# The old columns of a packed inverse: added by VectorE in strips, instead of through a product with the identity

## The chip, the cores and the metric

One core of a Trainium2 chip runs the whole program. The metric is the device time of one execution in microseconds, and kernels are compared by the median of several executions.

## The reference

The kernel computes one decoder layer with two groups of heads: four heads of gated delta-rule linear attention, and four heads of differential attention. The change lies in the first group. Its sequence of 2048 positions is cut into chunks (64 in the reference, 128 in the kernel, which gives the same result), and each chunk needs a unit lower triangular system solved:

```python
m = jnp.where(strict, jnp.einsum('bhncd,bhnsd->bhncs', k_beta, kc) * decay, 0.0)
lmat = m + jnp.eye(CHUNK, dtype=m.dtype)
rhs = jnp.concatenate([v_beta, k_beta * jnp.exp(gc)[..., None]], axis=-1)
sol = lax.linalg.triangular_solve(lmat, rhs, left_side=True, lower=True,
                                  unit_diagonal=True)
u, w = sol[..., :dv], sol[..., dv:]
```

Then a scan over the chunks carries the state, and the outputs of both groups go through one output projection and are added to the input.

## The kernel before, in words

The program has two stages. In the first, `feed` (L878) issues the input projections (tiles `pct` and `pnat`, each of 24 products of split operands, L365 and L384), while `gdn` (L909) runs the delta-rule units: `gdn_unit` (L596) prepares one head for 512 positions, that is four chunks of 128, and `gdn_scan` (L802) carries the state through them. There are 16 units in two chains, `gg` 0 and 1, which run side by side. `mingle` (L137) lays some steps of the projections between any two steps of the units. In the second stage `attention` (L1166) runs the differential attention, mingled with the output projection (`outp`). From what is written, a scheduler with a clock of its own makes the order in which each engine gets its instructions; each engine then takes them strictly in that order. Every matmul is recorded at L130 and every transpose at L133, so they are told apart by their tiles.

A unit inverts its four unit triangular 128x128 matrices `L` by doubling: it starts with the inverses of 2x2 blocks, and each level joins pairs of blocks into blocks of twice the size. At a level, only the odd half of each pair's columns of `N` (the inverse so far, transposed) changes: the new columns are the old ones, plus a correction. Levels 1 to 4 (block sizes 2, 4, 8 and 16) stay within diagonal blocks of 32x32 and are computed *packed*: the 16 diagonal blocks of the four chunks are gathered into one 128x128 tile, `Nc` for `N` and `Lc` for `L`, where partition strip m of 32 holds the m-th diagonal blocks of all four chunks. For each packed level (L722 to L750):

- `xq` (L734): one product of `Lc` with the odd columns `No` of the full `N`, 256 columns; VectorE masks it into `X` (L736).
- `nq` (L739, L740): two products of 256 columns into the same PSUM tile. The first, with the identity `identr` as stationary operand, copies `No` into it; the second adds the correction, `TT` times `X` (`TT` is the packed `N` transposed). The mask's sign makes the correction negative.
- VectorE writes `No` from `nq`, times a mask that keeps the diagonal blocks (L741, 128x256), and ScalarE copies the four strips of `nq` into `Nc` (L744, four copies of 32x64), except at the last packed level.
- `tp` (L707): `Nc` is transposed and ScalarE copies it to `TT` for the next level (L709). After the last packed level the four chunks of `N` itself are transposed (L715, L717), for the two wide levels that follow.

The PSUM tiles `xq`, `nq` and `tp` of a chain are one buffer (`ua`, L316), so each waits until the one before it has been read.

The two lines that compute the old columns:

```python
PE.matmul(blocks(np_), lhsT=identr, rhs=No, start=True, stop=False)
PE.matmul(np_, lhsT=TT[:, 0, :], rhs=X, start=False, stop=True)
```

Of the kernel before, what the change touches and what calls it, by code (L numbers as in the profile page):

```python
# [13 lines left out]
ALU = mybir.AluOpType  # L14
AX = mybir.AxisListType

P = 128
# [6 lines left out]
NCH = 4  # L24
# [43 lines left out]
LEVELS = [1, 2, 4, 8, 16, 32, 64]  # L68


WIDE = (0, 5, 6)
PACKED = (1, 2, 3, 4)
PK = 32
NM = len(WIDE) * P + (len(PACKED) + 1) * 2 * P


def level_masks():

    s = np.arange(P)[:, None]
    c = np.arange(P)[None, :]  # L80

    def level(b, s, c):
        return (s // (2 * b) == c // (2 * b)) & (s // b % 2 == 0) & (c // b % 2 == 1)

    m = [level(LEVELS[i], s, c).astype(np.float32) for i in WIDE]
    j, k, i = np.meshgrid(np.arange(4), np.arange(4), np.arange(16), indexing="ij")
    for n in PACKED:
        b = LEVELS[n]
        col = (i // b * 2 * b + b + i % b).reshape(-1)[None, :]
        m.append(-((s // PK == j.reshape(-1)[None, :]) & level(b, s % PK, col)).astype(np.float32))  # L90
    m.append((s // PK == k.reshape(-1)[None, :]).astype(np.float32))
    return np.ascontiguousarray(np.concatenate(m, 1))


def f(ap):
    return ap.bitcast(F32)
# [3 lines left out]
def hybrid_kernel(  # L100
# [21 lines left out]
    V, A, PL, SY = nc.vector, nc.scalar, nc.gpsimd, nc.sync  # L122
# [12 lines left out]
    PE = Recorder()  # L135

    def mingle(a, b, rate, slack=0, drain=True):  # L137

        credit = 0.0
        steps = [None] * (slack + 1)  # L140
        done = object()
        while a or (b and drain):
            last[0] = None
            r = next(a, done) if a else "wait"
            if last[0]:
                steps = steps[1:] + last
            step = steps[0]
            credit = rate[0] if r else credit + rate[0]
            q = None
            while b and (credit > 0 or not a) and not q:  # L150
                with tc.issue_after(step.ins) if step else ExitStack():
                    q = next(b, done)
                credit -= 1.0
            assert not (r == "wait" and q == "wait"), "stuck"
            a = None if r is done else a
            b = None if q is done else b
        return b
# [90 lines left out]
    identr = const.tile([P, P], F32R, name="identr")  # L248
# [4 lines left out]
    PL.affine_select(utri, ones, pattern=[[1, P]], compare_op=ALU.is_ge, fill=0.0, base=0, channel_multiplier=-1)  # L253
    lmask = const.tile([P, NM], F32, name="lmask")
    ab = const.tile([P, 2, H], F32, name="ab")
# [60 lines left out]
    def ua(gg, name, dt=F32):  # L316
        return psg.tile([P, NCH, P], dt, tag=f"ua{gg}", name=name, bufs=1)
# [278 lines left out]
    def gdn_unit(h, g):  # L596
# [3 lines left out]
        s = {k: a[:, h, 4 * gg : 4 * gg + 4] for k, a in sc[hf].items()}  # L600

        def t(tag, name, dt=F32, shape=S4):
            return gp.tile(shape, dt, tag=f"u{gg}_{tag}", name=f"u{gg}_{name}")
# [40 lines left out]
        b = gp.tile([P, NCH], F32, tag="l_b", name="b", bufs=3)  # L644
# [45 lines left out]
        N = t("c", "N", F32R)  # L690
# [4 lines left out]
        Nc = t("Nc", "Nc", F32R, [P, NCH, PK])  # L695
        strips = [slice(PK * m, PK * m + PK) for m in range(NCH)]
# [4 lines left out]
        def flat(a):  # L701
            return a.rearrange("p a b -> p (a b)")

        def transposed_packed():

            tp = ua(gg, "tp", F32R)
            PE.transpose(tp[:, 0, :], flat(Nc), identr)  # L707
            TT = t("d", "TT", F32R)
            A.copy(TT[:, 0, :], f(tp[:, 0, :]))  # L709
            return TT  # L710

        def transposed(N):
            tp = ua(gg, "tp", F32R)
            for j in range(NCH):
                PE.transpose(tp[:, j, :], N[:, j, :], identr)  # L715
            TT = t("d", "TT", F32R)
            A.copy(TT, f(tp))  # L717
            return TT

        TT = transposed_packed()  # L720
        yield
        for i in PACKED:  # L722


            def half(a, lvl=LEVELS[i]):
                return a.rearrange("p (m two b) -> p m two b", two=2, b=lvl)[:, :, 1, :]

            def blocks(a, lvl=LEVELS[i]):
                return a.rearrange("p (m b) -> p m b", b=lvl)

            No = half(flat(N))
            off = len(WIDE) * P + PACKED.index(i) * 2 * P
            xp_ = flat(ua(gg, "xq")[:, :2, :])
            PE.matmul(blocks(xp_), lhsT=flat(Lc), rhs=No, start=True, stop=True)  # L734
            X = flat(t("e", "X", F32R)[:, :2, :])
            V.tensor_tensor(X, xp_, lmask[:, off : off + 2 * P], op=ALU.mult)  # L736
            yield
            np_ = flat(ua(gg, "nq")[:, :2, :])
            PE.matmul(blocks(np_), lhsT=identr, rhs=No, start=True, stop=False)  # L739
            PE.matmul(np_, lhsT=TT[:, 0, :], rhs=X, start=False, stop=True)  # L740
            V.tensor_tensor(No, blocks(np_), blocks(lmask[:, NM - 2 * P :]), op=ALU.mult)  # L741
            if i < PACKED[-1]:
                for m, r in enumerate(strips):
                    A.copy(  # L744
                        Nc.rearrange("p j (m two b) -> p j m two b", two=2, b=LEVELS[i])[r, :, :, 1, :],
                        np_.rearrange("p (j k m b) -> p j k m b", j=NCH, k=NCH, b=LEVELS[i])[r, :, m],
                    )
            yield
            TT = transposed_packed() if i < PACKED[-1] else transposed(N)
            yield  # L750
        for i in WIDE[1:]:

            def odd(a):
                return a.rearrange("p j (m two b) -> p j m two b", two=2, b=LEVELS[i])[:, :, :, 1, :]
# [4 lines left out]
            No = odd(N)  # L759
# [4 lines left out]
            X = t("e", "X", F32R)[:, :, :HC]  # L764
            V.tensor_tensor(blocks(X), blocks(xp_), odd(lm(i)), op=ALU.mult)
            yield
            np_ = ua(gg, "np")[:, :, :HC]
# [4 lines left out]
            TT = transposed(N)  # L772
# [136 lines left out]
    def gdn():  # L909


        def chain(gg):
            for hf in range(2):
                for h in range(H):
                    n = 8 * hf + 2 * h + gg
                    while ready[0] <= n or scanned[0] < n - 2:
                        yield "wait"
                    yield from gdn_unit(h, 2 * hf + gg)
# [413 lines left out]
    b = mingle(gdn(), behind(), pace, SLACK, drain=False)  # L1332
# [34 lines left out]
```

## Time and profile before

| | |
|---|---|
| median of 3 runs | 1680.2 us (1675.32 to 1682.49) |
| the profiled execution's own time | 1688.5 us |
| its span, first to last instruction | 1686.8 us |
| mean granted TensorE clock | 0.976 of full speed |
| instructions | 27350 |

The profiled execution is a run of its own, 0.5% above the median of the others; durations and waits are taken from it. Engines are named PE (TensorE's matmuls), PEld (its weight loads), DVE (VectorE), ACT (ScalarE), POOL (GpSimd) and SP. A row names an instruction by line, engine, operation and the tiles out<-in, where the numbers of tiles are left out: `u_N` is `N` of a unit of either chain. A matmul's duration in a row overlaps that of its neighbours; what it takes of TensorE's time is the step from its start to the next one's.

### The profile page before, as it was taken

How to read it: one execution, taken by the hardware profiler on the slowest of the kernel's cores; microseconds unless marked ns; L12 is line 12 of the kernel's file. 1: busy time of each engine (PE TensorE's matmuls, PEld its weight loads, DVE VectorE, ACT ScalarE, POOL GpSimd, SP SyncE). 2: the span in 40 equal slices, each digit the busy share in tenths (PEclk: the TensorE clock that was granted, in tenths of full speed). 3: DMA queues.
4: the chain of work that ended last, by engine and by line, in shares of the span. 5: the costliest groups of instructions: out<-in, count | busy, mean ns of one | idle time of the engine just before them, and what ended most of it. 6: DMA issues, size and time to landing. Idle time of an engine off the chain costs nothing.

```text
span 1686.8 us, 27350 instructions
## 1 busy us (share of the span) xinstructions
PE 1584.1 (94%) x9388; PEld 1374.7 (82%) x9388; DVE 1067.4 (63%) x2435; ACT 788.4 (47%) x2409; POOL 697.7 (41%) x846
## 2 busy tenths in 40 slices
PE   5999999999998999999999999889999989998997
PEld 4888898888987988898889898678778767777876
DVE  3765666746444684756654543338888768888872
ACT  4444444343345444334434343337777555565540
POOL 2464375352352347257442352213333353443343
PEclk8999999999999999999999999899999989999999
DMA  7342245233336432424422322896653364743344
GB/s 171 74 101 63 54 86 124 51 96 56 77 99 134 83 92 72 73 57 107 107 59 73 49 71 70 195 265 199 185 150 112 114 175 132 187 137 108 98 159 156
DMA packets 187703, 188.51 MB, mean 112 GB/s; under 512 B 12978, under 2 KB 143148, under 8 KB 187564
## 3 DMA queue, kind: packets, MB, share of 16 engines
q1 hardware_dynamic: 187564, 186.76, 43.6%
q8 instruction: 74, 1.21, 0.3%
q14 instruction: 65, 0.53, 0.1%
HBM read 124.82 MB, written 61.90 MB: 111 GB/s over the span
## 4 chain that ended last, share of the span: by engine, by line
PE 73%; DVE 10%; DMA 7%; ACT 3%; POOL 3%; issue 2%; SPq 1%; DVEq 0%; ACTq 0%; POOLq 0%
PE pct L130 25%; PE pnat L130 13%; PE outp L130 8%; PE oT L130 6%; PE sp L130 5%; PE wtp L133 2%; DVE nm L1024 2%; DMA u_gcr<-gc_d 2%; DMA wor<-in_w_out_dram 2%; DVE ex L1078 1%; PE gqp L130 1%; PE op L130 1%; PE ysp L130 1%; ACT ex L1026 1%; DVE qkraw L510 1%
## 5 line engine op out<-in xcount | busy, mean ns | idle before, releaser
L1026 ACT ACTIVATE ex<-sp,nm 128x512 f32<-128x512 f32 (+3 forms) x320 | 198.5, 625 | 100.2 <-DVE nm L1024 82.4
L130 PE MATMUL outp<-wo,mt 128*128 128x512 f32 x720 | 205.7, 416 | 10.8 <-ACT wo L1203 5.2
L1024 DVE TENSOR_REDUCE nm<-sp 128x1 f32<-128x512 f32 (+3 forms) x320 | 186.8, 602 | 26.4 <-PE sp L130 24.8
L130 PE MATMUL sp<-k,qs 128*128 128x512 f32 (+3 forms) x640 | 184.3, 393 | 19.0 <-ACT ex L1026 17.9
L130 PEld LDWEIGHTS outp<-wo,mt 128*128 128x128 f32 x720 | 130.2, 192 | 35.7 <-ACT wo L1203 5.9
L130 PE MATMUL pnat<-wh_fqk,xh 128*128 128x256 f32 (+1 forms) x512 | 152.9, 300 | 5.5 <-DVE xl L342 2.5
L130 PE MATMUL pnat<-wl_fqk,xh 128*128 128x256 f32 (+1 forms) x512 | 151.4, 297 | 1.3 <-POOL wl_fqk L361 1.3
L130 PE MATMUL pnat<-wh_fqk,xl 128*128 128x256 f32 (+1 forms) x512 | 150.5, 295 | 0.0
L130 PEld LDWEIGHTS sp<-k,qs 128*128 128x128 f32 x640 | 107.5, 191 | 47.9 <-ACT ex L1026 35.2
L1074 POOL TENSOR_SCALAR ex<-ex,al 128x512 f32<-128x512 f32 (+3 forms) x140 | 94.5, 691 | 95.6 <-ACT al L1035 92.3
L130 PE MATMUL oT<-wt,v 128*128 128x256 f32 (+1 forms) x576 | 132.6, 374 | 1.4 <-ACT wt L1084 1.4
L564 DVE SCALAR_TENSOR_TENSOR cy<-craw,cc,cy 128x512 f32<-128x512 f32 x144 | 124.0, 862 | 3.3
L130 PEld LDWEIGHTS oT<-wt,v 128*128 128x128 f32 x576 | 108.3, 193 | 17.7 <-ACT wt L1084 2.4
L1078 DVE SCALAR_TENSOR_TENSOR ex<-ex,cf 128x512 f32<-128x512 f32 (+3 forms) x160 | 111.2, 739 | 9.7 <-ACT cf L1053 9.2
L130 PEld LDWEIGHTS pnat<-wh_fqk,xh 128*128 128x128 f32 x512 | 100.7, 197 | 7.5 <-issue 2.6
L130 PE MATMUL pct<-xh,wh_dvz 128*128 128x512 f32 x256 | 104.1, 407 | 0.0
L130 PE MATMUL pct<-xl,wh_dvz 128*128 128x512 f32 x256 | 103.5, 404 | 0.0
L130 PE MATMUL pct<-xh,wl_dvz 128*128 128x512 f32 x256 | 103.5, 405 | 0.0
L130 PEld LDWEIGHTS pnat<-wl_fqk,xh 128*128 128x128 f32 x512 | 100.9, 197 | 2.3 <-POOL wl_fqk L361 1.7
L130 PE MATMUL pct<-xh,wh_dqk 128*128 128x512 f32 x256 | 102.3, 399 | 0.0
L130 PE MATMUL pct<-xl,wh_dqk 128*128 128x512 f32 x256 | 102.1, 399 | 0.0
L130 PEld LDWEIGHTS pnat<-wh_fqk,xl 128*128 128x128 f32 x512 | 100.9, 197 | 0.3
(280 smaller groups left out, 4132.4 us busy)
## 6 DMA issues: line engine op xcount, KB each, us to landing
qs<-qst_d SPq DMA_DIRECT2D x128, 128.0 KB, 3.8
mt<-mx_d SPq DMA_DIRECT2D x48, 256.0 KB, 4.8
k<-kst_d SPq DMA_DIRECT2D x40, 256.0 KB, 6.2
wr_dqk<-in_w_in_dram SPq DMA_DIRECT2D x32, 256.0 KB, 5.0
wr_dvz<-in_w_in_dram SPq DMA_DIRECT2D x32, 256.0 KB, 6.0
qst_d<-qkhl SPq DMA_DIRECT2D x16, 512.0 KB, 2.8
kst_d<-qkhl SPq DMA_DIRECT2D x16, 512.0 KB, 7.8
part_d<-xr SPq DMA_DIRECT2D x32, 256.0 KB, 4.1
```

The lines of the kernel that those rows point to most:

```text
L130: last[0] = nc.tensor.matmul(*a, **k)
L133: last[0] = nc.tensor.transpose(*a, **k)
L510: V.tensor_tensor(rv, rv, bc(r[:, j].unsqueeze(2), [P, 4, 64]), op=ALU.mult)
L564: V.scalar_tensor_tensor(y, raw[:, j : j + G], convc[:, j, idx : idx + 1], y, op0=ALU.mult, op1=ALU.add)
L1024: V.tensor_reduce(mx, sp[:, :w], axis=AX.X, op=ALU.max, negate=True)
L1026: A.activation(e[:, :w], sp[:, :w], AF.Exp, bias=mx, accum_out=ss[:, m, pi : pi + 1])
L1074: PL.tensor_scalar(e0[:, :w], e0[:, :w], al[:, 0, pi : pi + 1], 1.0, op0=ALU.mult, op1=ALU.mult)
L1078: V.scalar_tensor_tensor(e1[:, :w], e1[:, :w], cf[:, pi : pi + 1], e0[:, :w], op0=ALU.mult, op1=ALU.add)
```

## The change

The identity product and the block mask are gone. Now `nq` holds the correction alone, and VectorE adds it, strip by strip, to the packed `Nc` in place: four instructions of 32x64 at every packed level, the last one too. Then ScalarE copies the four strips from `Nc` into the odd columns of the full `N`, again four instructions of 32x64, at every packed level. So the transposition of `Nc` waits for VectorE instead of ScalarE, and whatever reads `N` (the next level's `xq`, and after the last packed level the four transposes of `N`) waits for the ScalarE copies that stand behind VectorE's adds. The mask table is 256 columns narrower.

```diff
--- before.py
+++ after.py
@@ -71,7 +71,7 @@
 WIDE = (0, 5, 6)
 PACKED = (1, 2, 3, 4)
 PK = 32
-NM = len(WIDE) * P + (len(PACKED) + 1) * 2 * P
+NM = len(WIDE) * P + len(PACKED) * 2 * P
 
 
 def level_masks():
@@ -83,12 +83,11 @@
         return (s // (2 * b) == c // (2 * b)) & (s // b % 2 == 0) & (c // b % 2 == 1)
 
     m = [level(LEVELS[i], s, c).astype(np.float32) for i in WIDE]
-    j, k, i = np.meshgrid(np.arange(4), np.arange(4), np.arange(16), indexing="ij")
+    j, _, i = np.meshgrid(np.arange(4), np.arange(4), np.arange(16), indexing="ij")
     for n in PACKED:
         b = LEVELS[n]
         col = (i // b * 2 * b + b + i % b).reshape(-1)[None, :]
         m.append(-((s // PK == j.reshape(-1)[None, :]) & level(b, s % PK, col)).astype(np.float32))
-    m.append((s // PK == k.reshape(-1)[None, :]).astype(np.float32))
     return np.ascontiguousarray(np.concatenate(m, 1))
 
 
@@ -736,15 +735,17 @@
             V.tensor_tensor(X, xp_, lmask[:, off : off + 2 * P], op=ALU.mult)
             yield
             np_ = flat(ua(gg, "nq")[:, :2, :])
-            PE.matmul(blocks(np_), lhsT=identr, rhs=No, start=True, stop=False)
-            PE.matmul(np_, lhsT=TT[:, 0, :], rhs=X, start=False, stop=True)
-            V.tensor_tensor(No, blocks(np_), blocks(lmask[:, NM - 2 * P :]), op=ALU.mult)
-            if i < PACKED[-1]:
-                for m, r in enumerate(strips):
-                    A.copy(
-                        Nc.rearrange("p j (m two b) -> p j m two b", two=2, b=LEVELS[i])[r, :, :, 1, :],
-                        np_.rearrange("p (j k m b) -> p j k m b", j=NCH, k=NCH, b=LEVELS[i])[r, :, m],
-                    )
+            PE.matmul(np_, lhsT=TT[:, 0, :], rhs=X, start=True, stop=True)
+
+            for m, r in enumerate(strips):
+                nb = np_.rearrange("p (j k m b) -> p j k m b", j=NCH, k=NCH, b=LEVELS[i])[r, :, m]
+                c = Nc.rearrange("p j (m two b) -> p j m two b", two=2, b=LEVELS[i])[r, :, :, 1, :]
+                V.tensor_tensor(c, f(c), nb, op=ALU.add)
+            for r in strips:
+                A.copy(
+                    N.rearrange("p j (m two b) -> p j m two b", two=2, b=LEVELS[i])[r, :, r.start // (2 * LEVELS[i]) : r.stop // (2 * LEVELS[i]), 1, :],
+                    f(Nc).rearrange("p j (m two b) -> p j m two b", two=2, b=LEVELS[i])[r, :, :, 1, :],
+                )
             yield
             TT = transposed_packed() if i < PACKED[-1] else transposed(N)
             yield
```

How the orders move. In these pieces names carry the scheduler's numbers where they tell units apart; `u0` and `u1` are the two chains.

On TensorE, around the first packed level of the chain-0 unit of the second head (`nq` at 240.2 us of the trace). Before:

```order
L133 MATMUL qktp<-ident,qkraw 128x128
L130 MATMUL pnat<-wh_fqk_0_2255,xl_411 128x256
L130 MATMUL pnat<-wh_fqk_0_2255,xh_410 128x256
L130 MATMUL nq<-u_N,identr 128x256
L130 MATMUL nq<-u_X,u_TT 128x256
L130 MATMUL pnat<-wl_fqk_0_2256,xh_410 128x256
```

Now:

```order
L132 MATMUL qktp<-ident,qkraw 128x128
L129 MATMUL pnat<-wh_fqk_0_2279,xl_411 128x256
L129 MATMUL pnat<-wh_fqk_0_2279,xh_410 128x256
L129 MATMUL nq<-u_X,u_TT 128x256
L129 MATMUL pnat<-wl_fqk_0_2280,xh_410 128x256
```

The identity product is gone and nothing takes its place; the projections around it close up.

On TensorE, at the last packed level of the chain-1 unit of the third head (403 to 406 us of the trace). Before:

```order
L133 MATMUL tp_4577<-identr_171,u0_N_4181 128x128 x4
L130 MATMUL nq_4567<-u1_N_4215,identr_171 128x256
L130 MATMUL nq_4567<-u1_X_4539,u1_TT_4520 128x256
L130 MATMUL pct_4631<-xh0_221,wh_dvz3_0_4360 128x512
...
L130 MATMUL pct_4631<-xl0_222,wh_dvz3_0_4364 128x512
L133 MATMUL tp_4589<-identr_171,u1_N_4215 128x128 x4
```

Now:

```order
L129 MATMUL pct_4629<-xh1_410,wl_dqk3_0_4406 128x512
L129 MATMUL nq_4633<-u1_X_4599,u1_TT_4580 128x256
L129 MATMUL pct_4703<-xh0_221,wh_dvz3_0_4412 128x512
...
L129 MATMUL pct_4703<-xh0_221,wl_dvz3_0_4413 128x512
L132 MATMUL tp_4649<-identr_171,u0_N_4229 128x128 x4
L129 MATMUL pct_4703<-xh0_221,wh_dvz3_0_4416 128x512
...
L129 MATMUL pct_4703<-xl0_222,wh_dvz3_0_4416 128x512
L132 MATMUL tp_4661<-identr_171,u1_N_4263 128x128 x4
```

The left-out rows are projection products: eleven of them stood between the level's product and the four transposes of the unit's `N`, and now eleven and the four transposes of the other chain's `N`, which stood ahead of the product before.

On ScalarE, around 271 us of the trace, where a chain-0 unit is at its last packed level and the chain-1 unit at its first two. Before:

```order
L744 CAST u_Nc<-nq 32x32x2 x4
L500 COPY qkraw<-pnat 128x256
L709 CAST u_TT<-tp 128x128
L500 COPY qkraw<-pnat 128x256
L360 CAST wh_dqk_0_3262<-wr_dqk_0_3259 128x2x256
L479 ACTIVATE qkhl<-qktp,qg 128x512
L744 CAST u_Nc<-nq 32x16x4 x4
L500 COPY qkraw<-pnat 128x256
L717 CAST u_TT<-tp 128x512
```

Now:

```order
L745 CAST u_N<-u_Nc 32x4x8x2 x4
L499 COPY qkraw<-pnat 128x256
L708 CAST u_TT<-tp 128x128
L499 COPY qkraw<-pnat 128x256
L745 CAST u_N<-u_Nc 32x4x16 x4
L499 COPY qkraw<-pnat 128x256
L745 CAST u_N<-u_Nc 32x4x4x4 x4
L359 CAST wh_dqk_0_3304<-wr_dqk_0_3301 128x2x256
L478 ACTIVATE qkhl<-qktp,qg 128x512
L716 CAST u_TT<-tp 128x512
```

Copies out of `nq` (L744) have become copies from `Nc` to `N` (L745) at the same places, and a block of four more (`32x4x16`, the last packed level) stands ahead of the copy `u_TT` of 512 columns that follows the transposes of `N`.

## Rows read from the trace of the kernel before

**Rows 1.** Busy time by stage: us, length, then each engine's busy time, clock, DMA.
```profile
core 0: us, PE busy (x) PEld busy (x) DVE busy (x) ACT busy (x) POOL busy (x), PEclk, DMA share, GB/s
95.00:1062.00 967.00, 939.78 (x6026) 841.48 (x6025) 551.36 (x1146) 392.55 (x1188) 431.11 (x478) 0.99 0.35 80
1062.00:1100.00 38.00, 28.01 (x164) 23.45 (x162) 13.62 (x34) 12.21 (x30) 11.43 (x10) 0.87 0.97 232
1100.00:1687.00 587.00, 541.65 (x2786) 444.13 (x2786) 442.67 (x1102) 338.15 (x1072) 217.37 (x311) 0.97 0.53 155
```

**Rows 2.** The chain of waits from 95 to 1062 us, shares by line.
```profile
by line: PE pct L130 41.3%; PE pnat L130 20.9%; DMA u_gcr<-gc_d 3.1%; PE gqp L130 2.3%; PE op L130 2.1%; PE ysp L130 2.1%; DVE qkraw L510 1.8%; PE tp L133 1.7%; PE nq L130 1.7%; PE wp L130 1.3%; issue 1.3%; PE rp L130 1.2%; POOL qkr L507 1.
```

**Rows 3.** Groups by line and shape: count | busy us, mean ns | idle before.
```profile
L744 ACT CAST u_Nc<-nq 32x64 fp32r<-32x64 f32 x192 | 39.3, 205 | 31.6 <-DVE u_N L741 27.6
...
L741 DVE TENSOR_TENSOR u_N<-nq,lmask 128x256 fp32r<-128x256 f32 x64 | 26.7, 420 | 36.1 <-PE nq L130 35.9
...
L130 PE MATMUL nq<-u_N,identr 128*128 128x256 f32 x64 | 21.9, 343 | 1.9 <-DVE u_X L736 1.8
...
L698 ACT CAST u_Lc<-u_L 32x128 fp32r<-32x128 f32 x64 | 18.9, 295 | 0.6
...
L796 DVE TENSOR_TENSOR Ub<-ubp,b 128x512 f32<-128x512 f32 x16 | 11.0, 688 | 20.8 <-PE ubp L130 20.8
...
L650 DVE TENSOR_TENSOR u_rki<-u_ssn,u_rr 128x4 f32<-128x4 f32 x16 | 2.9, 181 | 0.0
```

**Rows 4.** Timeline of a first packed level: start us, length us, instruction, idle before.
```profile
145.74 0.43 PE L130 MATMUL nq<-u_N,identr 128*128 128x256 f32 x1
...
145.99 0.30 PE L130 MATMUL nq<-u_X,u_TT 128*128 128x256 f32 x1
...
146.13 0.28 PE L130 MATMUL pnat<-wl_fqk,xh 128*128 128x256 f32 x1
...
146.32 0.43 DVE L741 TENSOR_TENSOR u_N<-nq,lmask 128x256 fp32r<-128x256 f32 x1 [2.06 <-PE nq L130]
...
146.84 0.91 ACT L744 CAST u_Nc<-nq 32x64 fp32r<-32x64 f32 x4
```

**Rows 5.** Timelines of a last level, of an inner level, of another last level.
```profile
403.26 0.39 PE L130 MATMUL nq<-u_N,identr 128*128 128x256 f32 x1
...
403.49 0.28 PE L130 MATMUL nq<-u_X,u_TT 128*128 128x256 f32 x1
...
404.88 0.41 DVE L741 TENSOR_TENSOR u_N<-nq,lmask 128x256 fp32r<-128x256 f32 x1
...
406.15 0.46 PE L133 MATMUL tp<-identr,u_N 128*128 128x128 f32 x4
...
670.34 0.28 PE L130 MATMUL pnat<-wh_fqk,xl 128*128 128x256 f32 x1
...
670.46 0.28 PE L130 MATMUL nq<-u_N,identr 128*128 128x256 f32 x1
...
670.58 0.28 PE L130 MATMUL nq<-u_X,u_TT 128*128 128x256 f32 x1
...
1042.83 0.42 DVE L741 TENSOR_TENSOR u_N<-nq,lmask 128x256 fp32r<-128x256 f32 x1 [4.52 <-PE nq L130]
...
1045.06 0.46 PE L133 MATMUL tp<-identr,u_N 128*128 128x128 f32 x4
```

**Rows 6.** TensorE waits, 95 to 1062 us: total us, times, longest.
```profile
PEld qktp L133 <- DVE qkraw L510: 7.6, 12, 2.4
...
PEld tp L133 <- ACT u_Nc L744: 3.0, 4, 1.8
...
PE tp L133 <- ACT u_Nc L744: 0.5, 1, 0.5
```

**Rows 7.** Timeline of VectorE, two instructions that follow each other.
```profile
203.32 0.68 DVE L785 TENSOR_TENSOR u_NF<-u_N,cp 128x512 f32<-128x512 f32 x1
203.92 0.68 DVE L637 TENSOR_TENSOR u_Kg<-knp,ts_eg 128x512 f32<-128x512 f32 x1
```

**Rows 8.** The chain of waits from 95 to 1062 us, two of its longest pieces.
```profile
540.69 6.46 DMA xt<-in_x_dram
...
961.76 9.06 DMA u_gcr<-gc_d
```

## Prediction

> **What bounds the kernel now.** I read the stages first. From 95 to 1062 us, the stretch that holds the projections and the delta-rule units, TensorE is busy 939.8 of 967.0 us at a granted clock of 0.99 of 2.4 GHz, VectorE 551 and ScalarE 393 [rows 1]. So TensorE sets the pace there, the other two have four tenths and more of the time free, and only 27 us of TensorE idle time are left to be won or added to. The chain of waits over that stretch says the same: pct and pnat, the projections, hold 62% of it, and the products nq, the only place where the identity product runs, hold 1.7%, or 16.4 us [rows 2]. From 1062 to 1100 us TensorE waits for weights (28.0 of 38 us busy, DMA at 0.97), and from 1100 us on, in attention, it is busy 541.7 of 587 us [rows 1]. Every packed level is done by 1070 us. A TensorE microsecond saved before 1062 us should move the rest forward, since the weight loads behind that stretch start when its buffers come free.
>
> **The identity product, removed.** There are 64 (16 units, 4 levels), and the mean record is 343 ns [rows 3]. That isn't the price: records overlap, and what counts is the step from one start to the next. Where plain work surrounds the pair the step is 0.12 us (670.46 to 670.58), the same as a projection product of 256 columns before it (670.34 to 670.46) [rows 5]. At the first packed level, whose columns lie in runs of two, it is 0.25 us (145.74 to 145.99) [rows 4], and right behind a short wait 0.23 us (403.26 to 403.49) [rows 5]. Part of such a long step is a start-up that the product left behind will then pay itself. I take 0.22 for the 16 first levels and 0.14 for the other 48: 3.5 + 6.7 = **10.2 us**. Bounds: all at 0.12 gives 7.7, all at 0.23 gives 14.7. The chain agrees with the middle: of 16.4 us on nq, 64 kept products at 0.12 take 7.7, and 8.7 remain [rows 2].
>
> **The strips on VectorE, and the copies on ScalarE.** Before, one VectorE instruction writes N (420 ns, x64), and then four ScalarE copies bring the strips to Nc (205 ns, x192) [rows 3]. After, four VectorE adds of 32x64 write Nc (256 in all) and four ScalarE copies write N (256, at the last level too). No VectorE strip stands in the trace. From 512 to 256 columns out of PSUM a two-input instruction falls from 688 to 420 ns, 1.05 ns a column, so 64 columns would take about 0.22 us; the bounds are the 181 ns of a 128x4 one and the 420 ns of the whole [rows 3]. I take 0.22, nearest in operands: 256 x 0.22 - 26.7 = 29.6 us more for VectorE (20 to 81 by the bounds). A scalar copy of 32x64 from SBUF lies between 205 ns (same size, from PSUM) and 295 ns (32x128, from SBUF); at 0.25 ScalarE gets 64 - 39.3 = 25 us more [rows 3]. Both lie beside TensorE's work: of 967 us VectorE would be busy 581, ScalarE 418.
>
> **Which waits move.** In the level shown, the product starts at 145.99, VectorE writes N from 146.32 to 146.75, and only then do the copies run, 146.84 to 147.75: Nc is complete 1.4 us after VectorE could begin [rows 4]. Now it is complete after four adds, 4 x 0.22 = 0.9 us. The transpose of Nc comes 0.5 us sooner, which can take back the 3.5 us (3.0 + 0.5) that TensorE spent on that wait [rows 6]; I take 2 us gained, 0 to 3.5. N is complete later: 0.9 us of adds and the tail of the copies behind them, about 2 us in place of 0.4. At the first three levels N is read by the next xq, which the old order puts far behind the transpose, so I cost that at nothing; its cover is the projection products between them, and without them it would be 1.5 us a level. At the last level the four transposes of N follow sooner. One had 0.86 us in hand (N written at 405.29, read at 406.15), another 1.81 (1043.25, 1045.06) [rows 5]; 1.5 us more delay makes the first 0.6 us late and the second not at all. Over 16 units I take 2 us lost; the bounds are 0 and 16 x 1.5 = 24. The new order softens it: in 10 of the 16 units more instructions stand between the last product and those transposes than before, in 3 fewer.
>
> **VectorE's queue.** Its largest wait in the stretch is TensorE's for qkraw, 7.6 us [rows 6]; with 5% more work on VectorE I add 1 us of waiting, 0 to 6. Against the strips stands a rule of the queue. The trace shows that two full-height VectorE instructions overlap: one of 0.68 us starts at 203.32, the next at 203.92, 0.08 earlier than its end [rows 7]. The Trainium skill (VectorE: DVE Perf Modes, "Two Vector instructions with no wait between them") says that an instruction is held until all earlier ones have finished when it starts in another group of 32 partitions than the last. No run here shows it yet; each strip would be such a case, and my sum already counts strips at full length, without overlap.
>
> **The rest.** The mask table loads 256 columns less, early and beside other transfers: nothing. **Sum:** -10.2 - 2 + 2 + 1 = **-9.2 us** of the profiled execution's 1688.5, or -0.54%. That execution is 0.5% above the median of 1680.2, so the share is applied to the median: **1671.0 us**.
>
> **Rivals.**
> *A. The step is only the stream.* If every long step is a start-up that the kept product inherits, 64 x 0.12 = 7.7 us is saved, the other terms stay, and the time is 1673.5: no change that can be told, since about 0.5% (8.4 us) is what a measurement of this kernel can tell from none. For it: the even steps at 670 us [rows 5]. Against: 0.25 us at a first level with plain products around it [rows 4]. The Trainium skill (TensorE: Matmul & The Clock Gate, "Wait — 56ns, not 53.3ns?") goes further this way: N / 2.4 GHz plus 2.5 ns a product, 109 ns for 256 columns, which as an estimate makes it 7.0 us; the trace's plain step is 0.12.
> *B. The saving is swallowed.* The units are one long chain of small steps, and the chain of waits holds pieces that no product shortens: 6.5 us for an x tile, 9.1 us for gcr [rows 8]. If such waits grow by what TensorE gives back, some 0 to 4 us remain: 1676 to 1680. Against it: TensorE is 97% busy there.
> *C. Slower: the last level.* If the four copies stand behind other scalar work, each unit's transposes of N stop TensorE for the full 1.5 us and more: 24 us lost and 1 us in VectorE's queue against 12.2 won gives 1693. It decides from 0.7 us a unit on (the saving is gone), and by 1.2 us a unit the kernel is slower by 0.5%. For it: the tight case at 405 us; against: the looser one at 1043 [rows 5], and the transposes moved back.
> *D. Attention is dealt anew.* The scheduler orders instructions by its own clock, so attention's TensorE order changes too, though nothing in it was edited. Its 45 us of TensorE idle time [rows 1] could change by a fifth either way: 1662 or 1680.
>
> **Chances.** Forecast 0.42, A 0.14, B 0.18, C 0.12, D 0.14 (half each way). Faster by over 0.5% (under 1671.8): 0.36 of the forecast's 0.42, as its spread reaches over the line, 0.02 of A, 0.07 of D, 0.02 of B: 0.47. Slower: 0.11 of C. Within: 0.42. The range goes from D's lower end and the identity's upper price, 1660, to between B and C, 1687; what is left out is most of C and the far end of D.
>
> **What would show it.** Right: no identity product in the groups; 64 nq products; TensorE busy in the stretch before attention some 10 us less and that stretch shorter by as much; VectorE strips near 0.22 us x256, ScalarE copies near 0.25 us x256; almost no wait of the Nc transpose. Wrong: the four transposes of N waiting on ScalarE by more than 5 us in sum, or a stretch as long as before with more TensorE idle time, or an attention stage that changes by over 5 us.

## The result, and the profile after

The changed kernel takes **1671.9 us** (median of 20 runs, 1667.7 to 1676.8) against 1680.9 us before (20 runs, 1675.3 to 1686.4): a ratio of **0.9941**, interval 0.9930 to 0.9952, or some 10 us. The forecast was 1671.0. The two profiled executions took 1688.5 us (before, 8 us above its median) and 1676.8 us (after, 5 above), so their difference holds some 3 us that are not the change's; the experiments below are judged by medians, and the profiles are used for places. From first to last instruction the profiles differ by 11.7 us: 9.4 up to the last projection product, 3.3 from there to the first attention score, and 1.0 lost in attention.

The changed kernel by stage, cut as in [rows 1] up to 1100 us (columns as there):

```profile
95.00:1062.00 967.00, 937.03 (x5988) 837.37 (x5987) 576.20 (x1342) 418.45 (x1261) 432.55 (x481) 0.98 0.36 82
1062.00:1100.00 38.00, 29.10 (x162) 23.70 (x161) 13.75 (x35) 10.37 (x30) 10.84 (x9) 0.90 0.98 232
1100.00:1675.00 575.00, 531.60 (x2752) 435.88 (x2752) 439.50 (x1093) 334.48 (x1062) 219.04 (x309) 0.98 0.50 154
```

VectorE is at 576.2 us and ScalarE at 418.5, where the working had 581 and 418. The new groups, 95 to 1062 us (columns as in [rows 3]), and a level's strips and copies in the timeline:

```profile
L745 ACT CAST u_N<-u_Nc 32x64 fp32r<-32x64 f32 x256 | 62.2, 243 | 56.4 <-DVE u_Nc L743 48.7 <-POOL u_Nc L698 2.4
L743 DVE TENSOR_TENSOR u_Nc<-u_Nc,nq 32x64 fp32r<-32x64 f32 x256 | 55.5, 217 | 45.9 <-PE nq L129 36.7 <-PE pnat L129 2.0 <-ACT craw L558 0.9
```
```profile
240.08 0.96 DVE L743 TENSOR_TENSOR u_Nc<-u_Nc,nq 32x64 fp32r<-32x64 f32 x4
240.37 0.79 ACT L745 CAST u_N<-u_Nc 32x64 fp32r<-32x64 f32 x3 [0.69 <-DVE u_Nc L743]
```

A strip takes 217 ns, and four of them 0.96 us from the first start to the last end: none overlaps the next. A copy takes 243 ns. TensorE's waits for the two transposes of a unit (engine, line, waited for: us, times, longest):

```profile
PE tp L132 <- DVE u_Nc L743: 4.2, 6, 1.1
PE tp L132 <- ACT u_N L745: 1.0, 2, 0.7
...
PEld tp L132 <- issue: 3.2, 4, 1.4
...
PEld tp L132 <- ACT u_N L745: 1.9, 2, 1.1
```

The wait of the Nc transpose did not go, it grew. Before, TensorE stood twice for it: the 0.5 us of [rows 6], and at 137.7 us another 1.6, which the list puts down to another tile, although the weight load of `Nc` waits for `u_Nc` at the same moment (the 1.8 us in [rows 6]):

```profile
PE tp L133 <- DVE qkhl L480: 1.6, 1, 1.6
```

That makes 2.1 us, and now it is 4.2, at six moments; the weight loads still wait at all six, but the list puts that down to "issue" and to products. The transposes of N, which did not wait, now wait 1.0 us, and their weight loads 1.9 at the same two moments. The chain of waits over the stretch still lies on the projections, and the piece `u_gcr` is smaller than in [rows 2] (3.1%):

```profile
by line: PE pct L129 37.3%; PE pnat L129 23.0%; PE gqp L129 2.6%; PE op L129 2.3%; PE ysp L129 2.2%; DMA xt<-in_x_dram 2.1%; DMA u_gcr<-gc_d 2.0%; issue 1.9%; PE tp L132 1.8%; PE ubp L129 1.2%; DVE cy L563 1.2%; PE rp L129 1.2%; PE qktp L13
```

**One place.** Counted by projection products (there are 4224), the changed kernel is ahead by 1.6 us at the 1056th, behind by 3.5 at the 2640th, ahead by 1.9 at the 3696th and by 9.5 at the 3960th. Most of the lead appears between products 3828 and 3960. There the kernel before did this (SP's queue, VectorE, TensorE, 959 to 975 us):

```profile
961.30 0.37 SPq L354 DMA_DIRECT2D wr_fz<-in_w_in_dram  x1
961.76 0.46 SPq L610 DMA_DIRECT2D u_gcr<-gc_d  x1
```
```profile
962.83 0.69 DVE L779 TENSOR_TENSOR u_R<-ident,rp 128x512 fp32r<-128x512 f32 x1 [0.20 <-PE rp L130]
970.85 0.69 DVE L619 TENSOR_TENSOR u_df<-u_gcr,ts_gcl 128x512 f32<-128x512 f32 x1 [7.33 <-DMA u_gcr<-gc_d]
971.46 0.68 DVE L529 SCALAR_TENSOR_TENSOR zz<-zz,pct 128x512 f32<-128x512 f32 x1
```
```profile
967.61 0.28 PE L130 MATMUL pnat<-wh_fv,xh 128*128 128x256 f32 x1
972.20 0.58 PE L130 MATMUL pnat<-wh_fv,xh 128*128 128x256 f32 x1 [4.31 <-DVE zz L529]
972.57 0.41 PE L130 MATMUL pnat<-wl_fv,xh 128*128 128x256 f32 x1
972.79 0.41 PE L130 MATMUL pnat<-wh_fv,xl 128*128 128x256 f32 x1
```

A 512 KB weight load went out 0.46 us ahead of the 256 KB load of `u_gcr` (the decay exponents of the next unit) on the same queue, and `u_gcr` landed 9.1 us later; the median of its 16 loads is 3.2. VectorE stood 7.33 us at `u_df`, the gate product `zz` stood behind it in VectorE's queue, and TensorE waited 4.31 us for the PSUM buffer that `zz` reads. After the pause its products step by 0.21 us for some 5 us instead of 0.12: the granted clock was at the lower of its two levels. In the changed kernel the order is another (SP, VectorE):

```profile
962.39 0.39 SPq L353 DMA_DIRECT2D wr_fz<-in_w_in_dram  x1
965.70 2.54 SPq L609 DMA_DIRECT2D u_gcr<-gc_d  x2
```
```profile
961.25 0.69 DVE L528 SCALAR_TENSOR_TENSOR zz<-zz,pct 128x512 f32<-128x512 f32 x1 [2.10 <-ACT zz L527]
...
970.54 0.69 DVE L618 TENSOR_TENSOR u_df<-u_gcr,ts_gcl 128x512 f32<-128x512 f32 x1 [3.67 <-DMA u_gcr<-gc_d]
```

`zz` is done at 961.9 us, 5 us before VectorE begins to wait at `u_df`; the load goes 3.3 us behind the weights, and TensorE has no pause there: products 3828 to 3960 take 29.1 us instead of 35.2. Nothing of the edit lies in this place; the scheduler dealt it anew.

**The whole stretch.** A place is not the sum. TensorE's time from the first to the last projection product can be split into the steps of the projections, the steps of everything else, and waits (idle time before an instruction). Before, that is 763.7 + 244.0 + 36.2 us, and in the changed kernel 764.0 + 235.6 + 35.0. So 8.4 of the 9.2 us by which the stretch is shorter are steps that went, and 1.2 are waits. The 4.3 us of the pause are nearly all lost again in other waits; those of the transposes of Nc and N alone grew by 3.1. So the total came as forecast, and the question is whether the identity product carries it, or the deal, which is the order that the scheduler gave the engines.

### The profile page after: what moved, and what is told of

Same layout as the page of the kernel before. It is cut to its first block, busy times and chain, and to the rows that moved or that the text cites. A ratio compares the mean times of both kernels' runs of the same rounds, so it can differ in the third digit from the quotient of the medians.

```text
span 1675.1 us, 27661 instructions
## 1 busy us (share of the span) xinstructions
PE 1573.9 (94%) x9324; PEld 1363.7 (81%) x9324; DVE 1091.5 (65%) x2627; ACT 809.9 (48%) x2473; POOL 700.3 (42%) x846
## 4 chain that ended last, share of the span: by engine, by line
PE 73%; DVE 9%; DMA 7%; ACT 4%; POOL 3%; issue 3%; SPq 1%; DVEq 0%; ACTq 0%; POOLq 0%
PE pct L129 23%; PE pnat L129 15%; PE outp L129 8%; PE oT L129 6%; PE sp L129 5%; PE wtp L132 2%; DVE nm L1025 2%; DVE ex L1079 2%; ACT ex L1027 2%; PE gqp L129 2%; PE op L129 1%; PE ysp L129 1%; DMA xt<-in_x_dram 1%; DMA u_gcr<-gc_d 1%; DMA wor<-in_w_out_dram 1%
## 5 line engine op out<-in xcount | busy, mean ns | idle before, releaser
L129 PE MATMUL outp<-wo,mt 128*128 128x512 f32 x720 | 201.9, 413 | 8.9 <-ACT wo L1204 5.7
L1075 POOL TENSOR_SCALAR ex<-ex,al 128x512 f32<-128x512 f32 (+3 forms) x140 | 99.7, 727 | 56.1 <-ACT al L1036 55.6
L563 DVE SCALAR_TENSOR_TENSOR cy<-craw,cc,cy 128x512 f32<-128x512 f32 x144 | 120.4, 839 | 3.3
L129 PE MATMUL pct<-xh,wl_dqk 128*128 128x512 f32 x256 | 101.2, 398 | 0.0
```

The source lines that it names most:

```text
L129: last[0] = nc.tensor.matmul(*a, **k)
L563: V.scalar_tensor_tensor(y, raw[:, j : j + G], convc[:, j, idx : idx + 1], y, op0=ALU.mult, op1=ALU.add)
L1075: PL.tensor_scalar(e0[:, :w], e0[:, :w], al[:, 0, pi : pi + 1], 1.0, op0=ALU.mult, op1=ALU.mult)
```

## The experiments

Every run was timed beside the kernel before, and a difference in us below is the difference of the two ratios to it, times 1681.

**identity_back**, the changed kernel with the identity product put back into `nq`; the strips then copy:

```diff
-            PE.matmul(np_, lhsT=TT[:, 0, :], rhs=X, start=True, stop=True)
+            PE.matmul(blocks(np_), lhsT=identr, rhs=No, start=True, stop=False)
+            PE.matmul(np_, lhsT=TT[:, 0, :], rhs=X, start=False, stop=True)
...
-                V.tensor_tensor(c, f(c), nb, op=ALU.add)
+                V.tensor_copy(c, nb)
```

> The changed kernel with the identity product put back in front of each level's product; VectorE's strips copy the sum to the packed form instead of adding, so everything behind TensorE stays as changed. Theory (the identity's own TensorE steps, 11.1 us in the trace of before, are what the change won): the saving is given back, +8 to +11 us on the changed kernel, 1680 to 1683 us, ratio to before 1.00. Rival (the saving came from the other order and the other waits, not from TensorE's work): 1672 us or so, ratio 0.994 to before.

1675.4 us, ratio 0.9955 (0.9938 to 0.9971). Only 2.4 us of the gain go, with an uncertainty of some 3. So a kernel that still has all 64 identity products is 7.5 us faster than before. In its profile the work did come back: TensorE's steps outside the projections are 243.9 us, 8.3 more than in the changed kernel. But its waits are 30.0 us, 5.0 fewer, and the projections' steps 757.8, 6.2 fewer, at the lower granted clock for 33 us of the stretch instead of 44 (its execution lies 3 us below its median, that of the changed kernel 5 above).

**identity_twice**, the kernel before with the identity product issued twice:

```diff
+            PE.matmul(blocks(np_), lhsT=identr, rhs=No, start=True, stop=True)
             PE.matmul(blocks(np_), lhsT=identr, rhs=No, start=True, stop=False)
```

> The kernel before with the identity product issued twice at each packed level (the second overwrites the first, so the result stays). Theory: the doubled product costs what the removed one did, +8 to +11 us, 1689 to 1692 us, ratio 1.005 to 1.0065. Rival (only its streaming counts, a start-up is shared with its neighbour): +7.5 us, 1688 us. Rival (swallowed by waits elsewhere): 1681 to 1684 us, ratio 1.000 to 1.002.

1705.5 us, ratio 1.0141 (1.0116 to 1.0167): +24 us, two to three times what was expected. The steps of the identity products, start to next start, sum to 20.6 us instead of 11.1, as they should. The rest lies elsewhere: from the first attention score to the end of TensorE's last product it takes 572.0 us instead of 562.6, though nothing there was edited. The run also tells what makes the step long at a first level. At a first packed level and at a later one, the two identity products, and the product behind them:

```profile
239.63 0.63 PE L130 MATMUL nq<-u_N,identr 128*128 128x256 f32 x2
240.08 0.30 PE L130 MATMUL nq<-u_X,u_TT 128*128 128x256 f32 x1
```
```profile
489.08 0.40 PE L130 MATMUL nq<-u_N,identr 128*128 128x256 f32 x2
489.32 0.28 PE L130 MATMUL nq<-u_X,u_TT 128*128 128x256 f32 x1
```

Two steps take 0.45 us where the columns lie in runs of two, and 0.24 where the runs are longer. At all 16 first levels the second product, right behind an equal one, steps by 0.23 to 0.24 us, so there the long step is not a start-up.

**last_direct**, the changed kernel with the last packed level added by VectorE directly into N; 64 ScalarE copies and the wait behind them are gone:

```diff
+                if i == PACKED[-1]:
+                    V.tensor_tensor(n, f(n), nb, op=ALU.add)
+                    continue
...
-            for r in strips:
+            for r in strips if i < PACKED[-1] else ():
```

> The changed kernel, but at the last packed level VectorE adds its strips to the full N directly, and the four ScalarE copies of that level are gone (64 in all, 15.6 us of ScalarE). Theory (the copies there cost TensorE 1 to 3 us of waiting for N): 1669 to 1671 us. Rival (the copies at the last level stop TensorE by 0.7 us and more in each of the 16 units): 1660 us or less. Rival (fully hidden): 1672 us.

1679.8 us, ratio 0.9977 (0.9962 to 0.9991): 6 us slower than the change, with less work. It reaches the last projection 5 us earlier (1047.5 against 1052.4 us), and then attention takes 572.4 us instead of 563.6 (all of it by one execution each).

**full_height**, the kernel before without the identity product: VectorE masks the correction into a scratch tile and adds that to N, two instructions of 128x256; ScalarE copies N to Nc:

```diff
-            PE.matmul(blocks(np_), lhsT=identr, rhs=No, start=True, stop=False)
...
-            V.tensor_tensor(No, blocks(np_), blocks(lmask[:, NM - 2 * P :]), op=ALU.mult)
+            C = flat(t("g", "C")[:, :2, :])
+            V.tensor_tensor(C, np_, lmask[:, NM - 2 * P :], op=ALU.mult)
+            V.tensor_tensor(No, f(No), blocks(C), op=ALU.add)
```

> The identity product removed from the kernel before in another way: VectorE masks the product into a scratch tile and adds that to N, two instructions of 128x256, and ScalarE then copies the strips from N to the packed form at the first three levels, as before but from SBUF. Theory (only the identity's steps on TensorE count, what evacuates it is hidden): as the changed kernel within 3 us, 1669 to 1675 us, ratio 0.993 to 0.997 to before. Rival (that the strips shorten the way to the packed transpose is part of the gain): the packed form is complete some 1.4 us later after each product than with strips, so TensorE waits at the transposes and the time is 1677 us or more.

1699.9 us, ratio 1.0096 (1.0073 to 1.0119): 16 us slower than before though the products are gone. The waits name the chain, 95 to 1090 us, and the groups show why it grew by more than one instruction:

```profile
PE tp L133 <- ACT u_Nc L745: 9.4, 11, 1.7
```
```profile
L742 DVE TENSOR_TENSOR u_N<-u_N,u_C 128x256 fp32r<-128x256 f32 x64 | 39.4, 620 | 1.7
L741 DVE TENSOR_TENSOR u_C<-nq,lmask 128x256 f32<-128x256 f32 x64 | 26.5, 418 | 31.4 <-PE nq L130 31.4
```

The add between two SBUF tiles takes 620 ns in the mean (median 425, longest 1506), and Nc is complete later. So where the old columns are added, and from where, is worth more than the product.

These four left two explanations of the sign of each result: the shorter way to Nc, or the deal. The next four were to part them.

**order_before** and **order_after**, memsets that nobody reads, one of 128x256 per unit in the kernel before, four in the changed one:

```diff
+        for _ in range(1):
+            V.memset(spare_t, 0.0)
         TT = transposed_packed()
```

> The kernel before, with one VectorE memset of 128x256 per unit into a tile that nobody reads: 16 instructions, some 3 us of VectorE in a stretch where it is over four tenths idle, no new wait. It does no harm by itself, but the scheduler deals TensorE's order anew: of the 1312 rows of attention 1171 keep their sequence, before attention 5221 of 5252. Theory 'order': edits that re-deal attention move the time by several us whatever they do, so this differs from the kernel before (1682) by 4 us or more in either direction. Theory 'mechanism' (the -9 us come from the strips and the identity): within 2 us of before, and attention's length within 2 us of 562.

> The changed kernel, with four VectorE memsets of 128x256 per unit into a tile that nobody reads (64, some 13 us of VectorE). Attention's TensorE order is dealt anew: of 1314 rows 1044 keep the sequence of the changed kernel and 966 that of the kernel before (767 between those two). Theory 'order': it loses much of the gain, 1675 to 1682. Theory 'mechanism': 1670 to 1675, as the edit of the strips is all there.

order_before: 1692.0 us, ratio 1.0062 (1.0048 to 1.0077), **+10.4 us for an edit that does nothing**. Its stretch to the last projection is not longer (1056.2 us); attention takes 571.9 us instead of 562.6. The loss is at its end: TensorE's longest waits there in order_before, and at the same tiles in before:

```profile
1635.59 0.69 PE L133 MATMUL aotp<-ident,aon 128*128 128x128 f32 x2 [4.86 <-DVE aon L1141]
1644.28 0.80 PE L130 MATMUL outp<-wo,mxl 128*128 128x512 f32 x1 [3.33 <-POOL mxl L852]
```
```profile
1640.22 0.41 PE L133 MATMUL aotp<-ident,aon 128*128 128x128 f32 x2 [1.44 <-DVE aon L1138]
...
1647.94 0.50 PE L130 MATMUL outp<-wo,mxl 128*128 128x512 f32 x1 [1.25 <-POOL mxl L849]
```

order_after: 1676.4 us, ratio 0.9972 (0.9960 to 0.9985), +5.2 us, just over the 1675 that theory 'mechanism' allowed. The memsets wait for nothing and run early, all 16 of order_before before 14 us of its trace and all 64 of order_after before 71, while the first product of a packed level comes at 131 us or later. So it is not their load that costs: the deal alone moves this kernel by as much as the change does.

**strips_spare** (the changed kernel, four VectorE instructions more per level, Nc + Nc into a spare tile) and **chain_longer** (two copies of Nc onto itself between the strips and the transpose):

```diff
+            for r in strips:
+                c = f(Nc)...[r, :, :, 1, :]
+                V.tensor_tensor(spare_t[r]..., c, c, op=ALU.add)
```
```diff
+            for _ in range(2):
+                V.tensor_copy(Nc, f(Nc))
```

> The changed kernel, with four more VectorE instructions of 32x64 at each packed level, which read the new columns of Nc and write a tile that nobody reads: 256 more, some 0.2 us each, +55 us of VectorE (577 to about 630 of 967 us), on no chain. It prices VectorE's load. My term: hidden, +1 us per 30 us, so +2 us (1674). Rival: VectorE's queue is on the chains (qkraw, xl, AT waits of TensorE), then +5 us or more (over 1677).

> The changed kernel, with two full-height VectorE copies of Nc onto itself (128x128) between the strips and the transpose of Nc: about 0.2 us each, so Nc is complete 0.4 to 0.5 us later at each of 64 levels, which is about the 1.35 us that the kernel before needed (0.42 us of VectorE and 0.91 of ScalarE); the load on VectorE grows by 26 us. Theory 'latency' (the shorter way from the product to the packed transpose is what gained): the transposes of Nc wait 8 us or more in sum instead of 4.0, and the time goes back by 5 to 9 us, 1677 to 1681. Theory 'identity or order': waits below 6 us, time within 2 us of 1672.

1717.8 us, ratio 1.0209 (1.0183 to 1.0235), and 1709.3 us, ratio 1.0161 (1.0140 to 1.0181): +45 and +37 us over the change, far beyond either theory. The durations of the added instructions were not the expected ones (first row strips_spare, second chain_longer):

```profile
L752 DVE TENSOR_TENSOR spare_t<-u_Nc 32x64 f32<-32x64 f32 x252 | 85.2, 338 | 7.2
```
```profile
L745 DVE CAST u_Nc<-u_Nc 128x128 fp32r<-128x128 f32 x128 | 52.2, 412 | 2.3
```

The medians are as expected, 217 and 227 ns; but 40 of 256 and 37 of 128 take over 300 ns, up to 1334 and 1323 ns, and every one of these ends within 0.1 us of the end of a GpSimd instruction. The strips of the change never take over 230 ns, though 134 of the 256 overlap a GpSimd instruction: they have one operand in PSUM. So the two runs do not price VectorE's load or 0.4 us of delay, as meant: chain_longer adds 0.8 us per level to the chain, strips_spare 1.4 us to VectorE's queue, with single delays of 1.3 us. What they do show is how short the change's slack is (first two rows chain_longer, the others strips_spare):

```profile
PE tp L132 <- ACT u_N L747: 15.5, 10, 3.9
PE tp L132 <- DVE u_Nc L745: 8.8, 8, 1.9
```
```profile
PE nq L129 <- DVE u_X L736: 9.9, 7, 4.0
PE tp L132 <- DVE u_Nc L744: 9.0, 10, 2.7
```

**identity_back2**, identity_back with a second identity product; **n_split**, two of the four N copies on GpSimd; **copies_spare**, four ScalarE copies more per level:

```diff
+            PE.matmul(blocks(np_), lhsT=identr, rhs=No, start=False, stop=False)
```
```diff
-            for r in strips:
-                A.copy(
+            for m, r in enumerate(strips):
+                (A.copy if m < 2 else PL.tensor_copy)(
```
```diff
+                A.copy(spare_t[r].rearrange("p j (m b) -> p j m b", b=LEVELS[i]), c)
```

> The changed kernel with the identity product put back twice (128 of them; VectorE copies the strips instead of adding; the second one doubles the old columns, so the numbers computed are others). Theory 'steps' (a product of 256 columns costs its step, 8 to 11 us per 64): with one put back the time was 1675.4, so 1683 to 1687, and TensorE's steps of identity products in the stage before attention sum to 18 to 22 us. Theory 'evacuation' (the identity costs some 2.4 us per 64, as the first put back did): 1677 to 1679.

> The changed kernel, with two of the four copies from Nc to N on GpSimd instead of ScalarE: 128 instructions of 32x64 move, ScalarE -31 us, GpSimd (431 us busy of 967) +30 to 60 us; N is complete some 0.5 us sooner where GpSimd is free. Theory 'N is late' (the longer copies chain cost the change part of its gain): the waits of the transposes of N on its copies, 2.9 us in the changed kernel, vanish, and the time is 1667 to 1671. Rival 'a third queue': GpSimd's own work stands ahead of the copies, these waits grow past 5 us, and the time is 1674 to 1685.

> The changed kernel, with four more ScalarE copies of 32x64 per packed level, which read Nc and write a tile that nobody reads: 256 more at 0.24 us, +62 us of ScalarE (418 to 480 of 967 us), no new wait of their own. Attention's TensorE order stays (1307 of 1314 rows keep their sequence), so attention should keep its length. It prices ScalarE's load as the spare strips did VectorE's (+57 us there cost 46). Theory 'any queue of the units is near its limit': 0.5 us and more per us, over 1700. Theory 'VectorE alone is': under 1680.

identity_back2: 1694.5 us, ratio 1.0075 (1.0055 to 1.0095), +20 us over identity_back. Its identity products take 20.7 us of steps instead of 11.0, so 9.7 us are theirs, and the place of the `u_gcr` load is back: products 3828 to 3960 take 34.5 us instead of 29.8. That makes 14. In the sums of the stretch, its steps outside the projections are 9.4 us more than identity_back's, its waits 5.3 and the projections' steps 2.8. n_split: 1682.7 us, ratio 1.0004 (0.9987 to 1.0021), 11 us slower; a GpSimd copy takes 296 ns, TensorE waits 3.7 us for these in place of 1.0, which does not explain 11, and its profiled run, 1678.3 us, was too fast to show the rest. copies_spare: 1687.9 us, ratio 1.0037 (1.0019 to 1.0054): 61 us of ScalarE cost 16, between the two theories.

**gcr_other_queue** changes the deal by one row. It is the kernel before, and ScalarE instead of SP issues the one `u_gcr` load of the place above; each engine's other instructions keep their order:

```diff
-        SY.dma_start(
+        (A if (h, g) == (H - 1, 2) else SY).dma_start(
```

> The kernel before, with one DMA issue moved: the u_gcr load of the last head's first unit of the second half (chain 0, issued at 961.76 us of the trace of before, 0.46 us behind the 512 KB weight load wr_fz on SP's queue, and landing 9.1 us later) is issued by ScalarE instead of SP. Every engine's order is otherwise the same, row for row; the identity products and the old evacuation stay. In before, and in the four other runs where the load stands behind wr_fz, VectorE waits over 7 us for it with the gate product zz behind it, TensorE waits 4.3 us for zz, and the 66 projection products from the 3828th on take some 22 us; in the eight runs where it does not, they take 15.7. Theory 'the stall carries most of the gain': the load lands within 6 us, TensorE's wait there falls below 2 us, those 66 products take 16 to 19 us, and the time is 1674 to 1678. Theory 'the stall is made up elsewhere': the wait falls and the time stays within 2 us of before's 1681. If the load still takes 9 us on the other queue, wait and time stay and nothing is told.

1681.6 us, ratio 1.0002 (0.9988 to 1.0015). The load went out at 958.79 us and VectorE began at:

```profile
967.08 0.69 DVE L619 TENSOR_TENSOR u_df<-u_gcr,ts_gcl 128x512 f32<-128x512 f32 x1 [6.25 <-DMA u_gcr<-gc_d]
```
```profile
968.43 0.39 PE L130 MATMUL pnat<-wh_fv,xh 128*128 128x256 f32 x1 [3.22 <-DVE zz L529]
```

Another queue did not help much: the load still took 8.3 us beside the weights, and 1.1 us less waiting is too little for the medians. That the place's 6 us reach the end is therefore not shown by taking them away from the kernel before. What is left is the table of all runs, worked out from the starts in each trace: identity products; from the first to the last projection product, TensorE's steps outside the projections, the projections' steps, and waits; us for products 3828 to 3960; start of the last projection product; from the first attention score to the end of TensorE's last product; median. All but the first and the last are of one execution each. gcr_other_queue has the order of the kernel before but for one load, and its execution still differs by 5 us at the last projection, 2 of them at the place, and by 3 in attention; so differences of a few us say little in these columns.

```
                 identity  other  proj.  waits  3828-3960  last proj.  attention  median
before               64  244.0  763.7   36.2      35.2      1061.8      562.6    1680.9
gcr_other_queue      64  244.6  760.6   33.0      33.0      1056.9      559.5    1681.6
order_before         64  244.1  759.4   34.4      34.1      1056.2      571.9    1692.0
full_height           0  240.5  764.4   47.7      35.0      1070.2      565.0    1699.9
identity_twice      128  253.0  766.2   35.3      34.8      1073.0      572.0    1705.5
identity_back2      128  253.3  760.6   35.3      34.5      1067.3      561.5    1694.5
after                 0  235.6  764.0   35.0      29.1      1052.4      563.6    1671.9
identity_back        64  243.9  757.8   30.0      29.8      1050.5      562.0    1675.4
order_after           0  234.6  762.9   35.0      29.3      1051.9      565.4    1676.4
last_direct           0  233.6  762.3   32.5      29.3      1047.5      572.4    1679.8
n_split               0  236.4  759.9   38.3      29.1      1052.5      558.7    1682.7
copies_spare          0  239.6  763.8   41.6      29.6      1063.4      564.5    1687.9
chain_longer          0  238.8  765.3   57.2      29.4      1079.3      551.0    1709.3
strips_spare          0  239.3  769.5   58.0      29.6      1085.8      564.2    1717.8
```

In the first six the `u_gcr` load goes 0.2 to 0.5 us behind `wr_fz`, in the other eight 3.3 us behind. full_height has the pause without any identity product, and identity_back has all 64 and no pause: the pause goes with the deal, and the identity product alone does not decide it. The steps outside the projections do go by the product, whatever the deal: 244 to 245 us with 64, 253 with 128, 234 to 236 with none (239 to 241 in the four kernels that lengthened the waits). The attention column parts by the deal again: 551 to 565 us, or 572 in three kernels, and none of them edits anything in attention.

## Why the prediction came out right, and which steps did not

**The identity's steps: the size was right, and in this pair it reached the end of the stretch.** Predicted 10.2 us (7.7 to 14.7). In the profiles 64 identity products took 11.1 us of steps, 3.8 at the first levels (3.5 taken) and 7.3 at the others (6.7), and the product left behind, without the waits behind it, grew from 8.6 to 10.2 us, so 9.5 went. A little of it was inherited, as rival A said, but not the long steps of the first levels (identity_twice). The stretch is 9.4 us shorter, as the signs of being right asked.

**What the prediction did not have: the rest is dealt anew.** It took a TensorE microsecond saved as one that moves the rest forward. That is not a rule here. Put back into the changed kernel, the same product brought 8.3 us of steps back, and only 2.4 us of time, with an interval that reaches from nothing to about 6, since the waits fell. Put in a second time it cost its 9.7 and more. That the waits of the two kernels sum to nearly the same, 36.2 and 35.0 us, is therefore luck: with the identity's work unchanged they lie between 30.0 and 36.2, and order_before loses 10.4 us by sixteen memsets. The row of 9.06 us on the `u_gcr` load [rows 8] was named as a wait that no product shortens (rival B); it is a product of the deal, and it moved, and other waits grew by nearly as much. What one identity product is worth in time in an unchanged order stays open, since no run kept the order.

**Strips and copies:** 217 ns (0.22 taken) and 243 ns (0.25 taken); VectorE and ScalarE as forecast. **The rule of the queue** that the Trainium skill states (VectorE: DVE Perf Modes, "Two Vector instructions with no wait between them") is now seen in this kernel: four strips in four partition groups take 0.96 us, without overlap, where two full-height instructions overlap by 0.08 us [rows 7]. The sum had counted them so.

**The Nc transpose: the step failed.** Nc is complete sooner, as said (0.96 us after VectorE begins instead of 1.4), but the 2 us were not gained, nor did the wait nearly vanish: TensorE waits 4.2 us in place of 2.1. The 3.5 us of the prediction had also added a matmul's wait of 0.5 us to one of its own weight load at the same moment, and left out the 1.6 that stood under another tile. Why an earlier Nc is waited for longer is not shown; TensorE's order around these transposes was dealt anew too.

**The last level:** 2 us lost were forecast; TensorE waits 1.0 us, and its loads 1.9 at the same two moments. Rival C did not come, but its mechanism is real: with 0.8 us more on the chain (chain_longer) these waits become 15.5 us.

**VectorE's queue:** +1 us was forecast for `qkraw`; that wait fell from 7.6 to 5.6 us. "Hidden" was too simple, though: 61 us more on ScalarE alone cost 16.

**Rival D** did not happen in this pair (562.6 and 563.6 us of attention), but its size, 9 us either way, was well taken: the inert order_before lost 9 us by it, and chain_longer's attention is 12 us shorter.

## What to carry to other kernels

Where a scheduler deals the order, time an inert edit first: here sixteen memsets moved the kernel by 0.6%, as much as the change, so a gain of that size is not yet a reason. Counting a product that both kernels have shows the place where a lead appears, but add up steps and waits over the whole stretch before you credit that place: here a pause of 4.3 us went, other waits grew by nearly as much, and what left in sum was the product's steps. Putting the work back is no price either, as long as the order moves with it. And a VectorE step that stands on a chain was safer here with one operand in PSUM, where GpSimd is busy.

## What the runs showed of the hardware that was not expected

A VectorE instruction whose operands all lie in SBUF can be held by a running GpSimd instruction: in chain_longer one of 227 ns took 1.32 us, until the end of a GpSimd subtraction of 128x512 that had begun 0.08 us before it (VectorE, then GpSimd, whose row holds two):

```profile
170.88 1.32 DVE L745 CAST u_Nc<-u_Nc 128x128 fp32r<-128x128 f32 x1
```
```profile
170.80 3.18 POOL L360 TENSOR_TENSOR wl_dvz<-wr_dvz,wh_dvz 128x512 fp32r<-128x512 f32 x2 [0.76 <-ACT wh_dvz L359]
```

The Trainium skill says so (SBUF — State Buffer, "Who interferes with whom"): a VectorE instruction with two SBUF inputs, or a copy in a mode that uses both ports, takes a port that GpSimd also uses, and whichever starts later waits to the end of the other; one with at most one SBUF input, outside such a mode, does not. The runs agree in the main: 40 of 256 spare strips and 37 of 128 copies were held, and of the strips from PSUM none, with 230 ns the longest in the changed kernel. But not every GpSimd instruction holds: 34 spare strips took no more than 300 ns though one was running when they began, 25 of them beside `qkr` of 128x16, which takes some 2.9 us; why is not shown. ScalarE's spare copies, all in SBUF, were never held either (248 ns the longest of 256).

A load of 256 KB that goes 0.5 us behind one of 512 KB on the same queue landed after 9.1 us, where 3.2 is its median; from another queue it took 8.3.
